# Output projection in seven block products, and the second token half first into the norm and the up projection, in a hybrid attention/SSM encoder block

## The chip, the cores and the metric

The kernel runs on one NeuronCore of a Trainium2 chip. The metric is the device time of one execution in microseconds (us). Five engines work side by side, each through its own list of instructions in order: PE (TensorE, the matmuls), DVE (VectorE), ACT (ScalarE), POOL (GpSimd) and SP (SyncE, which here only starts transfers). Matrix products write to PSUM banks; ACT or DVE carry them out.

## What is computed

1024 tokens of width 1024, with 16 meta tokens ahead of them, pass through one layer: a mixer of attention and a state-space model, its output projection, a residual, and then a norm and a gated convolution FFN. The part that is changed is the end of the mixer and the start of the FFN:

```python
def _mixer(xn, w_in, ..., w_o):
    ...
    merged = g[..., :D_MODEL] * y_a.astype(jnp.float32) + g[..., D_MODEL:] * y_s.astype(jnp.float32)
    return merged.astype(xn.dtype) @ w_o        # (tokens, 1024) @ (1024, 1024)

x = x + _mixer(_rmsnorm(x, g1), ...)
...
def _conv_ffn(xn, w_up, conv_w, conv_b, w_down):      # xn = _rmsnorm(x, norm_ffn_g)
    hid = xn @ w_up                                   # (tokens, 1024) @ (1024, 5632)
    hp = jnp.pad(hid, ((0, 0), (CONV_WIDTH - 1, 0), (0, 0)))
    conv = conv_b + sum(hp[:, j:j + seq_len] * conv_w[j] for j in range(CONV_WIDTH))
    val, gate = jnp.split(conv, 2, axis=-1)
    return (jax.nn.silu(gate) * val) @ w_down
```

All of it is float32. Of the meta tokens, the output projection needs only the last two, since the causal convolution reaches two tokens back.

## The kernel before

**How a float32 product is made.** Each operand is split in two: a rounded high part `hi` (type fp32r), and a low part `lo`, the operand minus `hi`. A product is three matmuls, hi times hi, hi times lo and lo times hi, summed in one PSUM bank. ACT makes `hi` by a cast and DVE or POOL makes `lo` by a subtraction (`split_lo`, recorded as L128 whatever calls it).

**The order.** The code is recorded once; the build's scheduler and the buffers of each pool then settle each engine's list, so that the lists are not the code line by line. Within a list an instruction that waits holds all behind it.

**The stages around the change**, in order of time:
- *Attention*, four pairs of heads. In these stages POOL makes masks, scalings and weight casts, and some transfers start on its queue.
- *Merge* (L907 on). For each of eight chunks i of 128 features, 36 matmuls multiply attention output by `w_ao`; DVE multiplies by the gate (L916) and adds the state-space part `mi` (L917); ACT casts the 128x1026 sum to `xhi`, and POOL makes `xlo`. POOL also casts the weights of a coming chunk (`whi`, L148) here.
- *Output projection* (L931 on). For two halves of 512 output columns, and for each of 8 tiles of 128 tokens, 24 matmuls of 512 columns give one bank; DVE adds it to `h2` (L955). The two meta tokens take 16 more matmuls per half (`stacked`). The split weights `woh`, `wol` come from `wo_half` (ACT cast, DVE subtraction of 128x1024), four loads of 512 KB for each half.
- *Norm*, tile by tile in the second half: ACT squares and sums, DVE forms the variance `vr`, POOL its power (`rs`, L172), DVE scales to `xs` (L177), PE transposes (L185), ACT casts to `xhi` (L187) and DVE makes `xlo`.
- *Up projection* (L1039 on). `plain_pair(0)` computes the first of 22 channel pairs: two row blocks, each in three pieces of 342 tokens with 24 matmuls each; ACT and twice DVE (L1057) carry a piece out with the convolution's taps. `xn_forms()` then makes the sums of token halves that later block products need (POOL L1072, DVE L252 to L256, and splits), `plain_pair(1)` follows, and then `block` pairs (L213 to L215 on PE), each in seven products. The weights of every pair are loaded, cast on ACT (L1002) and split on DVE.
- *Down projection*, which uses seven block products too, with operands formed on POOL, ACT and DVE.

The weights for the down projection have sums of blocks made in DRAM while other work runs: SP copies a block to `t_d` and a POOL transfer adds another (L1028).

## Time and profile before

| | |
|---|---|
| median of 3 runs | 1508.7 us (1506.5 to 1511.5) |
| the profiled execution | 1509.3 us, of which the span from first to last instruction is 1507.5 us |
| mean granted TensorE clock | 0.989 of full |
| PE | busy 1454.5 us, 96% of the span, 9736 matmuls |
| DVE | busy 1064.2 us, 71% |
| POOL | busy 714.8 us, 47% |
| ACT | busy 679.0 us, 45% |

PE is busy nearly always, so a slice in which it is not, and what it waits for there, is what one looks for first. The stages of the change take some 220 us of the span: the merge from 664 to 710 us, the output projection and the norm to 823 us, `plain_pair(0)`, `xn_forms` and `plain_pair(1)` to 868.8 us, and the `block` pairs behind that. A matmul's busy time includes its run through the pipeline, so that the distance between two starts, the pitch, tells what one costs.

### The profile page before, as it was taken

To read this page: it belongs to the slowest core of one execution; us is meant where nothing else is said; L and a number is where in the kernel's file an instruction comes from. 1 tells how busy PE (TensorE), PEld (TensorE's weight loads), DVE (VectorE), ACT (ScalarE), POOL (GpSimd) and SP (SyncE) were. 2 spreads that over 40 slices of the span, in tenths; PEclk is the share of its full clock that TensorE was granted. 3 is DMA by queue.
4 is the path that set the end of the run, shared out by engine and by line. 5 is a ranking of instruction groups with operands and counts; after the bars stand their busy time and mean duration, and the time that the engine had idled before them with its cause. 6 is when DMAs were issued, how large, how long until landed. Compare 5 with 4: busy or idle time off the path is not lost.

```text
span 1507.5 us, 26382 instructions
## 1 busy us (share of the span) xinstructions
PE 1454.5 (96%) x9736; PEld 1366.9 (91%) x9736; DVE 1064.2 (71%) x2143; ACT 679.0 (45%) x1304; POOL 714.8 (47%) x805
## 2 busy tenths in 40 slices
PE   7999998999999999999999899999999999989997
PEld 6989997998999999999778899999999999878886
DVE  7878758871657676656255988888887775788785
ACT  6344665531646565532033444444444444444343
POOL 1411135760545555525011644555544326599766
PEclk9999999999999999999999999999999999999998
DMA  6465562551021202157241136766643214864413
GB/s 242 99 161 140 142 139 80 159 166 46 21 77 54 78 23 93 43 174 264 96 165 59 54 107 162 196 188 180 166 114 96 77 62 164 309 218 131 132 49 112
DMA packets 82245, 189.92 MB, mean 126 GB/s; under 512 B 14090, under 2 KB 24970, under 8 KB 81764
## 3 DMA queue, kind: packets, MB, share of 16 engines
q1 hardware_dynamic: 66164, 154.49, 31.4%
q0 software_dynamic: 9728, 23.09, 8.4%
q10 hardware_dynamic: 6224, 10.65, 1.9%
q8 instruction: 77, 1.26, 0.3%
q14 instruction: 52, 0.43, 0.1%
HBM read 149.12 MB, written 60.96 MB: 139 GB/s over the span
## 4 chain that ended last, share of the span: by engine, by line
PE 74%; DVE 13%; issue 3%; POOL 3%; DMA 3%; ACT 3%; SPq 0%; POOLq 0%; DVEq 0%; ACTq 0%
PE mm L154 5%; PE mm L156 5%; PE mm L155 5%; PE sp L214 3%; PE sp L213 3%; PE sp L215 3%; PE tp L750 2%; DVE sw L128 2%; PE tp L213 2%; PE tp L214 2%; PE tp L215 2%; DVE ov L1093 2%; PE mm L213 2%; PE mm L215 2%; PE mm L214 2%
## 5 line engine op out<-in xcount | busy, mean ns | idle before, releaser
L154 PE MATMUL mm<-xhi,whi 128*128 128x342 f32 (+2 forms) x488 | 159.4, 327 | 1.0 <-DVE q L128 1.0
L156 PE MATMUL mm<-xhi,wlo 128*128 128x342 f32 (+2 forms) x488 | 158.3, 325 | 0.0
L155 PE MATMUL mm<-xlo,whi 128*128 128x342 f32 (+2 forms) x488 | 157.6, 323 | 0.0
L128 DVE TENSOR_TENSOR sw<-sf,sw 128x512 fp32r<-128x512 f32 x76 | 75.8, 997 | 55.1 <-ACT sw L1002 55.1
L1033 POOL TENSOR_TENSOR ov<-ov,og 128x1024 f32<-128x1024 f32 x21 | 51.2, 2440 | 129.6 <-ACT og L1032 126.8
L1002 ACT CAST sw<-sf 128x512 fp32r<-128x512 f32 x76 | 47.5, 624 | 111.4 <-POOL sf L1010 79.6
L154 PEld LDWEIGHTS mm<-xhi,whi 128*128 128x128 f32 x488 | 91.9, 188 | 2.1 <-PE sp L708 0.8
L156 PEld LDWEIGHTS mm<-xhi,wlo 128*128 128x128 f32 x488 | 91.8, 188 | 0.3
L155 PEld LDWEIGHTS mm<-xlo,whi 128*128 128x128 f32 x488 | 91.9, 188 | 0.2
L213 PE MATMUL mm<-xhi,sw 128*128 128x256 f32 (+1 forms) x304 | 85.6, 282 | 1.0 <-DVE ov L1057 1.0
L215 PE MATMUL mm<-xhi,sw 128*128 128x256 f32 (+1 forms) x304 | 85.5, 281 | 0.0
L214 PE MATMUL mm<-xlo,sw 128*128 128x256 f32 (+1 forms) x304 | 85.2, 280 | 0.0
L757 ACT CAST th<-tp 128x256 fp32r<-128x256 f32 (+3 forms) x120 | 56.0, 472 | 61.8 <-PE tp L750 29.0
L128 DVE TENSOR_TENSOR tl<-tp,th 128x256 fp32r<-128x256 f32 (+3 forms) x120 | 65.2, 547 | 25.7 <-ACT th L757 24.4
L1002 ACT CAST sw<-raw 128x512 fp32r<-128x512 f32 x69 | 42.3, 620 | 79.8 <-DMA raw<-in_w_up_dram 36.5
L1093 DVE SCALAR_TENSOR_TENSOR ov<-hv,cwt,ov 128x1024 f32<-128x1024 f32 x38 | 77.5, 2040 | 0.3 <-ACT ov L1091 0.3
L722 POOL TENSOR_SCALAR pt<-pt,nm 128x144 f32<-128x144 f32 (+4 forms) x72 | 50.7, 706 | 53.8 <-DVE nm L721 52.4
L1010 POOL TENSOR_TENSOR sf<-raw,sf 128x512 f32<-128x512 f32 x38 | 64.0, 1683 | 23.2 <-DVE sw L128 23.1
L1010 POOL TENSOR_TENSOR sf<-raw 128x512 f32<-128x512 f32 x38 | 50.1, 1318 | 48.4 <-DVE sw L128 24.1
L172 POOL TENSOR_TENSOR rs<-vr,nhalf 128x1 f32<-128x1 f32 (+2 forms) x18 | 10.9, 605 | 113.9 <-DVE vr L170 61.5
L720 ACT ACTIVATE pt<-pt,nm 128x144 f32<-128x144 f32 (+4 forms) x72 | 52.9, 735 | 26.0 <-DVE nm L719 25.5
L713 DVE CUSTOM_DVE_ANT_0 pt<-sp,fb 128x328 f32<-128x328 f32 (+8 forms) x112 | 46.4, 430 | 20.6 <-PE sp L708 12.3
(606 smaller groups left out, 5648.9 us busy)
## 6 DMA issues: line engine op xcount, KB each, us to landing
raw<-in_w_up_dram SPq DMA_DIRECT2D x44, 512.0 KB, 3.9
t_d<-in_w_dn_dram POOLq DMA_DIRECT2D x44, 256.0 KB, 6.7
ar<-a_d SPq DMA_DIRECT2D x44, 256.0 KB, 4.3
wr<-t_d SPq DMA_DIRECT2D x44, 256.0 KB, 2.8
a_d<-ov SPq DMA_DIRECT2D x21, 512.0 KB, 2.6
wr<-in_w_dn_dram SPq DMA_DIRECT2D x33, 256.0 KB, 3.4
t_d<-in_w_dn_dram SPq DMA_DIRECT2D x22, 256.0 KB, 4.5
t_d<-t_d SPq DMA_DIRECT2D x22, 256.0 KB, 4.5
```

The costliest lines, as they stand in the source:

```text
L128: return eng.tensor_tensor(out_, src, hi.bitcast(F), ALU.subtract)
L154: yield PE.matmul(ps, whi[:, i, :], ahi[:, i], start=(i == 0), stop=False)
L155: yield PE.matmul(ps, whi[:, i, :], alo[:, i], start=False, stop=False)
L156: yield PE.matmul(ps, wlo[:, i, :], ahi[:, i], start=False, stop=(i == k - 1))
L213: PE.matmul(ps, a[0][:, i], bh, start=(i == 0 and not joins), stop=False, skip_group_check=True)
L214: PE.matmul(ps, a[0][:, i], bl, start=False, stop=False, skip_group_check=True)
L215: PE.matmul(ps, a[1][:, i], bh, start=False, stop=(i == kh - 1), skip_group_check=True)
L720: S.activation(pt[:n, :kc], pt[:n, :kc], AF.Exp, bias=nm[:n, 1:2], scale=0.125, accum_out=nm[:n, 2:3])
L757: S.copy(th[:kn, z:tw], tp[:kn, z:tw])
L1002: S.copy(hi, src)
L1010: sums.append(GP.tensor_tensor(f_, a, b, op))
L1093: V.scalar_tensor_tensor(out=o, in0=h_[:, j:SEQ + j], scalar=cwc(j, m), in1=o, op0=ALU.mult, op1=ALU.add)
```

## The change

The output projection is written as a 2 by 2 block product (token halves by feature halves by column halves) in seven products instead of eight, with sums of blocks as operands.

- **Products.** Each has 4 tiles of 128 tokens with 12 matmuls of 512 columns: 7 x 4 x 12 = 336, where there were 384. The meta tokens take four small products of 8 matmuls (32 as before). On PE the order is 0, 4, 1, 5, 2, 3, 6; products 4, 5 and 6 go on in the banks of 0, 1 and 3. DVE adds or subtracts each finished bank to `h2` (L1021 of after) and POOL adds product 2 to three more places, in 12 instructions.
- **Operands.** The eight merged tiles are kept in float32. POOL forms the token sums (16 of 128x512), ACT casts token and weight blocks of 128x512 (56), and the low parts are made on POOL for products 0, 4 and 5 and on DVE for 1, 2, 3 and 6. The operands of 0, 5 and 3 stand in the memory of `xhi`, those of 4 and 2 in that of `xlo`. `wo_half` is gone.
- **Weight sums.** Four blocks `to_d` of 512x512 are made in DRAM during the second and third pair of heads: four copies by SP and four accumulating transfers by POOL, 1 MB each.
- **Norm.** The last four token tiles are normed during product 6, then the meta tokens, then the first four tiles. The squares go into the buffer of `xs`.
- **Up projection.** `plain_pair(0)` is computed in two parts, each of two pieces of 254 to 258 tokens: the second token half, then the first. That is 192 matmuls of 256 to 260 columns, where there were 144 of 342 to 344.

The core of the diff:

```diff
+    def out_weight_sums(i, first):
+        steps = [[(3, o_block(0, 0), False), (1, o_block(0, 1), False)],
+                 [(3, o_block(0, 1), True), (1, o_block(1, 1), True)],
+                 [(2, to_d[3], False)], [(2, o_block(1, 1), True)], [(5, to_d[2], False)], [(5, o_block(1, 0), True)]]
+        for p, src, more in steps[i] if i < len(steps) else ():
+            d_ = GP.dma_start(to_d[p], src, accum_op=ALU.add) if more else SY.dma_start(to_d[p], src)
+            after(d_, first)
...
+    def out_forms(p, j):
+        a11, a21, a12, a22 = (merged[4 * k + j][:, 2 + 512 * h_:514 + 512 * h_] for k in range(2) for h_ in range(2))
+        sub, add = ALU.subtract, ALU.add
+        if p == 1:
+            GP.tensor_tensor(a11, a11, a21, sub)
+        elif p == 2:
+            GP.tensor_tensor(a11, a22, a11, add)
+        elif p == 3:
+            GP.tensor_tensor(a21, a22, a21, sub)
+        elif p == 6:
+            GP.tensor_tensor(a11, a11, a12, sub)
+        slot = slots_of[p][j]
+        for q, src in ((0, (a11, a11, a11, a21, a12, a22, a11)[p]), (2, wr.pop((p, j)))):
+            S.copy(slot[q], src)
+            split_lo(GP if p in (0, 4, 5) else V, slot[q + 1], src, slot[q])
...
         V.tensor_tensor(mi, mi, ga, ALU.add)
-        S.copy(xhi[:, i, T0:], mi)
-        split_lo(GP, xlo[:, i, T0:], mi, xhi[:, i, T0:])
-        if i == 1:
-            wo = [wo_half(wop, 0, mg, "wraw")]
+        out_forms((0, 4)[i // 4], i % 4)
...
-                for i in range(KD):
-                    PE.matmul(ps, xhi[:, i, t:t + n], woh[:, i], start=(i == 0), stop=False)
-                    PE.matmul(ps, xhi[:, i, t:t + n], wol[:, i], start=False, stop=False)
-                    PE.matmul(ps, xlo[:, i, t:t + n], woh[:, i], start=False, stop=(i == KD - 1))
-            V.tensor_tensor(dst[:, sl], ps[:n], dst[:, sl], ALU.add)
...
+        for i, (ah, al, bh, bl) in enumerate(slots_of[p]):
+            k_ = dict(skip_group_check=True)
+            PE.matmul(ps, ah[:, ts_], bh, start=(i == 0 and p not in JOINS), stop=False, **k_)
+            PE.matmul(ps, ah[:, ts_], bl, start=False, stop=False, **k_)
+            PE.matmul(ps, al[:, ts_], bh, start=False, stop=(i == 3), **k_)
+        if p == 0:
+            S.copy(to, ps)
+        else:
+            V.tensor_tensor(to, to, ps, ALU.subtract if p in MINUS else ALU.add)
+        if p == 2:
+            for d_, op in ((bot[:, l_], ALU.add), (bot[:, r_], ALU.subtract), (top[:, r_], ALU.subtract)):
+                GP.tensor_tensor(d_, d_, u2[t], op)
...
+    for p in (0, 4, 1, 5, 2, 3, 6):
+        for t in range(4):
+            out_product(p, t)
+            if p == 6:
+                normed(5 + t, h2[:, 4 + t], P)
...
+    normed(0, hm, 2)
+    for t in range(4):
+        normed(1 + t, h2[:, t], P)
...
-    plain_pair(0)
+    plain_pair(0, ([(514, 256), (770, 254)], [(0, 258), (258, 256)]))
     xn_forms()
     plain_pair(1)
```

**POOL in the merge stage.** Before, a weight cast `whi` and the low part of a merged chunk took turns:

```order
L148 TENSOR_SCALAR whi_8786<-raw_8784 128x512
L128 TENSOR_TENSOR xlo_91<-mi_8654,xhi_90 128x1026
L148 TENSOR_SCALAR whi_8841<-raw_8839 128x512
L128 TENSOR_TENSOR xlo_91<-mi_8727,xhi_90 128x1026
L148 TENSOR_SCALAR whi_8896<-raw_8894 128x512
```

In the changed kernel, in the same stage (`wr` is a raw weight block of the output projection, `mr` a merged tile, L931 a token sum for product 1, L935 one for product 3):

```order
L129 TENSOR_TENSOR xhi_94<-mr2_8510,xhi_94 128x512
L931 TENSOR_TENSOR mr2_8510<-mr2_8510 128x512
L149 TENSOR_SCALAR whi_8906<-raw_8904 128x512
L129 TENSOR_TENSOR xhi_94<-mr3_8511,xhi_94 128x512
L931 TENSOR_TENSOR mr3_8511<-mr3_8511 128x512
L149 TENSOR_SCALAR whi_8964<-raw_8962 128x512
L935 TENSOR_TENSOR mr0_8508<-mr4_8512,mr0_8508 128x512
L129 TENSOR_TENSOR xlo_95<-mr4_8512,xlo_95 128x512
L149 TENSOR_SCALAR whi_9018<-raw_9016 128x512
L935 TENSOR_TENSOR mr1_8509<-mr5_8513,mr1_8509 128x512
```

Token sums now stand between the weight casts on POOL.

**DVE at the end of the norm.** Before, the last low parts stand among the first evictions of `plain_pair(0)` (L1057), and the first subtraction of `xn_forms` (L252) follows:

```order
L128 TENSOR_TENSOR xlo_91<-sp_9698,xhi_90 128x4x128
L177 SCALAR_TENSOR_TENSOR xs_9739<-h2_9059,rs_9745,g2B_9082 128x1024
L128 TENSOR_TENSOR xlo_91<-tp_9705,xhi_90 128x4x128
L1057 SCALAR_TENSOR_TENSOR og_9799<-mm_9800,cwt_9770,og_9799 128x342 x2
L128 TENSOR_TENSOR xlo_91<-sp_9748,xhi_90 128x4x128
L128 TENSOR_TENSOR xlo_91<-tp_9755,xhi_90 128x4x128
L1057 SCALAR_TENSOR_TENSOR og_9799<-po_9828,cwt_9770,og_9799 128x342 x2
L252 TENSOR_TENSOR fb_9981<-fa_9980 128x514
```

In the changed kernel, at the same place (L1171 is the eviction, L254 the first subtraction):

```order
L129 TENSOR_TENSOR xlo_95<-sp_9847,xhi_94 128x4x128
L129 TENSOR_TENSOR xlo_95<-tp_9854,xhi_94 128x4x128
L1171 SCALAR_TENSOR_TENSOR og_9897<-mm_9898,cwt_9868,og_9897 128x256
L1171 SCALAR_TENSOR_TENSOR og_9897<-mm_9926,cwt_9868,og_9897 128x254
L1171 SCALAR_TENSOR_TENSOR og_9897<-mm_9898,cwt_9868,og_9897 128x256
L1171 SCALAR_TENSOR_TENSOR ov_9962<-mm_9963,cwt_9868,ov_9962 128x256
L1171 SCALAR_TENSOR_TENSOR og_9897<-mm_9926,cwt_9868,og_9897 128x254
L1171 SCALAR_TENSOR_TENSOR ov_9962<-po_9991,cwt_9868,ov_9962 128x254
L1171 SCALAR_TENSOR_TENSOR ov_9962<-mm_9963,cwt_9868,ov_9962 128x256
L1171 SCALAR_TENSOR_TENSOR ov_9962<-po_9991,cwt_9868,ov_9962 128x254
L254 TENSOR_TENSOR fb_10135<-fa_10134 128x514
```

All eight evictions of the second token half now stand behind the last low part and ahead of the first subtraction.

**DVE ahead of the norm.** In the changed kernel, after the low parts of product 3's operands, the up projection's weight splits (`sw`) stand among the evictions of product 2 (`u2`) and ahead of those of product 3 (`h2`), and the norm's `vr` and `xs` behind them:

```order
L1021 TENSOR_TENSOR u2_9077<-u2_9077,mm_9462 128x512
L129 TENSOR_TENSOR sw_9891<-raw_9889,sw_9891 128x512
L129 TENSOR_TENSOR sw_9894<-raw_9889,sw_9894 128x512
L129 TENSOR_TENSOR sw_9956<-raw_9954,sw_9956 128x512
L129 TENSOR_TENSOR sw_9959<-raw_9954,sw_9959 128x512
L1021 TENSOR_TENSOR u2_9077<-u2_9077,po_9463 128x512
L129 TENSOR_TENSOR sw_10208<-raw_10206,sw_10208 128x512
L129 TENSOR_TENSOR sw_10211<-raw_10206,sw_10211 128x512
L129 TENSOR_TENSOR sw_10301<-raw_10299,sw_10301 128x512
L129 TENSOR_TENSOR sw_10304<-raw_10299,sw_10304 128x512
L1021 TENSOR_TENSOR h2_9082<-h2_9082,mm_9537 128x512
L172 TENSOR_SCALAR vr_9620<-ss_9618 128x1
```

Before, such splits stood at the start of the norm too, among the evictions of the projection's second half:

```order
L128 TENSOR_TENSOR sw_10054<-raw_10052,sw_10054 128x512
L128 TENSOR_TENSOR sw_10057<-raw_10052,sw_10057 128x512
L170 TENSOR_SCALAR vr_9344<-ss_9342 2x1
L128 TENSOR_TENSOR sw_10147<-raw_10145,sw_10147 128x512
L955 TENSOR_TENSOR h2_9059<-mm_9363,h2_9059 128x512
L128 TENSOR_TENSOR sw_10150<-raw_10145,sw_10150 128x512
L177 SCALAR_TENSOR_TENSOR xs_9340<-hm_9084,rs_9346,g2B_9082 2x1024
L170 TENSOR_SCALAR vr_9393<-ss_9391 128x1
```

The splits keep their place at the head of the norm; ahead of product 3's evictions they are new.

## Rows read from the trace of the kernel before

**Rows 1.** The page: span, busy times of the engines.

```profile
span 1507.5 us, 26382 instructions
PE 1454.5 (96%) x9736; PEld 1366.9 (91%) x9736; DVE 1064.2 (71%) x2143; ACT 679.0 (45%) x1304; POOL 714.8 (47%) x805
```

**Rows 2.** Busy time by stretch of the span, us; columns in the first line.

```profile
core 0: us, PE busy (x) PEld busy (x) DVE busy (x) ACT busy (x) POOL busy (x), PEclk, DMA share, GB/s
440.00:460.00 20.00, 19.66 (x146) 18.76 (x145) 10.92 (x55) 10.30 (x32) 12.12 (x28) 1.00 0.28 85
...
664.00:710.00 46.00, 45.80 (x294) 45.52 (x292) 32.85 (x43) 12.57 (x13) 23.72 (x15) 1.00 0.71 233
710.00:814.00 104.00, 102.67 (x471) 81.55 (x472) 44.18 (x63) 26.15 (x45) 11.14 (x14) 1.00 0.36 133
...
829.00:878.00 49.00, 42.94 (x271) 42.39 (x270) 48.64 (x60) 24.57 (x42) 29.82 (x20) 0.93 0.20 55
...
986.00:1026.00 40.00, 40.00 (x339) 40.00 (x338) 33.09 (x42) 17.34 (x28) 21.93 (x19) 1.00 0.70 185
```

**Rows 3.** Timeline of PE: start us, duration us, instruction, [idle before <-releaser].

```profile
705.75 0.32 PE L915 MATMUL mm<-ohi,wlo 128*128 128x342 f32 x1
...
709.48 0.32 PE L915 MATMUL po<-ohi,wlo 128*128 128x342 f32 x1
710.50 0.48 PE L952 MATMUL po<-woh,xhi 128*128 128x512 f32 x1 [0.70 <-DVE gs L916]
710.81 0.40 PE L953 MATMUL po<-wol,xhi 128*128 128x512 f32 x1
...
715.93 0.40 PE L954 MATMUL po<-woh,xlo 128*128 128x512 f32 x1
...
822.21 0.60 PE L185 MATMUL sp<-ident,xs 128*128 128x128 f32 x4
822.64 0.60 PE L185 MATMUL tp<-ident,xs 128*128 128x128 f32 x4
...
859.14 0.62 PE L1051 MATMUL mm<-xhi,sw 128*128 128x344 f32 x1 [4.50 <-DVE og L1057]
```

**Rows 4.** Timeline of DVE at the end of the norm.

```profile
814.56 0.69 DVE L955 TENSOR_TENSOR h<-mm,h 128x512 f32<-128x512 f32 x1 [1.11 <-PE mm L954]
...
817.81 1.27 DVE L177 SCALAR_TENSOR_TENSOR xs<-h,rs,g2B 128x1024 f32<-128x1024 f32 x1
...
824.07 0.68 DVE L128 TENSOR_TENSOR xlo<-tp,xhi 128x512 fp32r<-128x512 f32 x1
...
829.32 1.78 DVE L252 TENSOR_TENSOR fb<-fa 128x514 f32<-128x514 f32 x1 [3.48 <-POOL fa L1072]
```

**Rows 5.** Groups of DVE and POOL, 655 to 845 us: busy us, mean ns | idle before.

```profile
L128 DVE TENSOR_TENSOR sw<-raw,sw 128x512 fp32r<-128x512 f32 x10 | 7.2, 742 | 4.1 <-ACT sw L1002 4.1
L1057 DVE SCALAR_TENSOR_TENSOR ov<-mm,cwt,ov 128x342 f32<-128x342 f32 x4 | 2.2, 563 | 0.0
...
L128 POOL TENSOR_TENSOR xlo<-mi,xhi 128x1026 fp32r<-128x1026 f32 x8 | 16.3, 2033 | 20.6 <-ACT xhi L918 20.6
L1072 POOL TENSOR_TENSOR fa<-xhi,xlo 128x514 f32<-128x514 f32 x6 | 8.5, 1437 | 7.5 <-DVE xlo L128 6.9 <-DVE t3l L128 0.6
L148 POOL TENSOR_SCALAR whi<-raw 128x512 fp32r<-128x512 f32 x7 | 8.2, 1175 | 15.4 <-PE po L155 13.0 <-PE mm L914 2.2
```

**Rows 6.** The same groups in the down projection, 1280 to 1508 us.

```profile
L128 DVE TENSOR_TENSOR op<-wr,op 128x512 fp32r<-128x512 f32 x15 | 19.4, 1301 | 1.1 <-ACT op L1159 1.1
...
L128 POOL TENSOR_TENSOR op<-wr,op 128x512 fp32r<-128x512 f32 x15 | 22.9, 1536 | 0.0
L1153 POOL TENSOR_TENSOR ar<-ar 128x512 f32<-128x512 f32 x11 | 17.1, 1561 | 5.4 <-DVE xlo L128 3.0 <-DVE xhi L128 2.5
```

**Rows 7.** Groups of POOL over the span: issue of its accumulating transfers.

```profile
L1028 POOL DMA_DIRECT2D t_d<-in_w_dn_dram x44 | 36.8, 1179 | 0.0
```

**Rows 8.** Timeline of POOL within the attention stage: a weight cast, scaling and split.

```profile
449.93 1.05 POOL L148 TENSOR_SCALAR whi<-raw 128x1024 fp32r<-128x1024 f32 x1 [2.33 <-PE mm L155]
450.95 1.05 POOL L440 TENSOR_SCALAR gs<-gs 128x1026 f32<-128x1026 f32 x1
451.98 2.38 POOL L128 TENSOR_TENSOR wlo<-raw,whi 128x1024 fp32r<-128x1024 f32 x1
```

More of the change, by code (lines that the diff above doesn't have):

```diff
@@ L930, in block_kernel @@
+    u2t = [n2.tile([P, 2, 512], F, tag="xs", name="u2", bufs=2) for _ in range(2)]
+    u2 = [t_[:, i] for t_ in u2t for i in range(2)]
+    hm = n2.tile([2, D], F, name="hm")
+    mstk = n2.tile([P, 12, 64], R, name="mstk")
+    md = n2.tile([P, 12, 2], F, name="md")
+    ml = n2.tile([2, 512], F, name="ml")
     h2 = n2.tile([P, KD, D], F, name="h2")
-    SY.dma_start(h2, x.rearrange("(c p) d -> p c d", p=P))
-    wop1 = pool(st_o, "wo1", side="right")
-    wo.append(wo_half(wop1, 1, wp, "raw"))
@@ new lines, in block_kernel, with meta_product @@
+    small = [n2.tile([P, 4, 512], R, name=f"op{q}") for q in range(4)]
+    slots_of[1] = slots_of[6] = [[t_[:, w] for w in range(4)] for t_ in small]
+    GP.memset(mstk.bitcast(F), 0.0)
+    for i in range(KD):
+        GP.tensor_copy(md[:, i], merged[i][:, :2])
+    GP.tensor_tensor(md[:, KD:], md[:, :4], md[:, 4:KD], ALU.subtract)
+    GP.tensor_copy(mstk[:, :, :2], md)
+    split_lo(GP, mstk[:, :, 32:34], md, mstk[:, :, :2])
+    HALF = [slice(0, 512), slice(512, D)]
+    def meta_product(ps, q, p, start=True, stop=True):
+        for i, (_, _, bh, bl) in enumerate(slots_of[p]):
+            PE.matmul(ps[:64], mstk[:, 4 * q + i], bh, start=start and i == 0, stop=False, skip_group_check=True)
+            PE.matmul(ps[:64], mstk[:, 4 * q + i], bl, start=False, stop=stop and i == 3, skip_group_check=True)
@@ new lines, in normed, with operands @@
+    def normed(c, dst, n):
+        xs = n2.tile([P, D], F, tag="xs", name="xs", bufs=2)
+        norm_rows(n2, dst, n, g2B, xs)
+        to_feature(xs, n, xhi, xlo, TILES[c][0] if c else T0)
+        if c:
+            SY.dma_start(h_d[P * (c - 1):P * c], dst)
+    after_of = {None: (1,), 0: (5,), 4: (2,), 5: (3, 6)}
+    tags = {1: "raw", 5: "whi", 2: "wlo", 3: "raw", 6: "whi"}
+    def operands(p):
+        for nx in after_of.get(p, ()):
+            for q in range(2):
+                out_weights(nx, q, wp, tags[nx])
+            for j in range(4):
+                out_forms(nx, j)
@@ new lines, in block_kernel @@
+    operands(None)
+    xc = x.rearrange("(c p) d -> p c d", p=P)
+    SY.dma_start(h2[:, :4], xc[:, :4])
+    for p in (0, 4, 1, 5, 2, 3, 6):
[3 more added lines that the diff above has]
+                normed(5 + t, h2[:, 4 + t], P)
+        if p == 0:
+            xy = t_ps()
+            meta_product(xy, 0, 0)
+            meta_out(xy, HALF[0])
+            GP.tensor_tensor(hm[:, HALF[1]], hm[:, HALF[1]], ml, ALU.subtract)
+        elif p == 4:
+            xy = t_ps()
+            meta_product(xy, 1, 4)
+            meta_out(xy, HALF[0])
+        elif p == 2:
+            xy = s_ps()
+            meta_product(xy, 1, 2, stop=False)
+        elif p == 3:
+            meta_product(xy, 2, 3, start=False)
+            meta_out(xy, HALF[1])
+        operands(p)
+        if p == 0:
+            SY.dma_start(h2[:, 4:], xc[:, 4:])
@@ L1037, in conv_out, with plain_pair @@
         return ha.tile([P, SEQ], F, tag=tag, name=tag)
[L1039 removed]
+    def plain_pair(c, parts=(QBLK,)):
         res = []
[L1041 to L1045 removed]
+        ws = {}
+        for part, (m, tag) in ((part, mt) for part in parts for mt in ((NFF + c, "og"), (c, "ov"))):
+            if m not in ws:
+                raw = up_raw(m)
+                ws[m] = [split_q(raw[:, KH * q:KH * q + KH]) for q in range(2)]
+                res.append(conv_out(m, tag))
+            w2, o = ws[m], res[len(ws) - 1 if len(ws) < 2 else int(m == c)]
+            for t, n in part:
                 w = min(n, SEQ - t)
@@ L1180, in banks @@
         return held[p]
-    HALF = [slice(0, 512), slice(512, D)]
     ss = {}
```

113 lines of the change are left out of this document (52 added, 61 removed).

## The prediction

> **What bounds the kernel now.** I read the page first: PE is busy for 1454.5 of 1507.5 us [rows 1], so the span shrinks where PE gets less to do, unless another engine takes over there. Next the busy time by stretch [rows 2]. In the merge stage (664 to 710 us) and in the output projection (710 to 814) PE is full, 45.80 of 46 and 102.67 of 104 us, while DVE has 32.85 and 44.18: PE bounds both. From 829 to 878 us it is the other way: DVE is busy 48.64 of 49 us, PE 42.94, at a granted clock of 0.93. Here `xn_forms` and the evictions of two plain pairs bound the kernel. The timelines show the same: PE waits 4.50 us at 859.14 for an eviction on DVE [rows 3], and DVE itself begins this work at 829.32, after 3.48 us of waiting for POOL's first sums [rows 4], which need the last low part of the norm (824.07 + 0.68 = 824.75).
>
> So the change takes its matmuls from a stretch that PE bounds, but just behind it stands one that DVE bounds, and whose start depends on the end of the norm. What counts is how much earlier the last low part is ready.
>
> **PE's own sum.** Starts of 512-column matmuls are (715.93 - 710.81) / 22 = 0.2327 us apart [rows 3]. 416 such matmuls become 368: 48 x 0.2327 = 11.2 us less. `plain_pair(0)` has 192 matmuls instead of 144. The 342-column pitch is (709.48 - 705.75) / 24 = 0.1555, the pitch near 256 columns 40.00 / 339 = 0.118 [rows 2, 3]: 22.7 against 22.4 us, 0.3 more. The 0.70 us of idle at 710.50 [rows 3], a wait for the last gated chunk, goes, since product 0 needs chunks 0 to 3 alone. PE alone would thus gain 11.2 + 0.7 - 0.3 = 11.6 us.
>
> **When the last low part is ready.** The merge ends at 709.8 (709.48 + 0.32). Up to product 6 PE has (6 x 48 + 32) x 0.2327 = 74.5 us, so that product 6 starts at 784.3. It takes 11.2 and the transposes of two token tiles, each two groups of (822.64 - 822.21) = 0.43 to 0.44 us [rows 3], 0.88 in all: 797.2. Then follow the transposes of two more tiles (1.8), the first part of `plain_pair(0)` (96 x 0.118 = 11.3) and, among its matmuls, those of the meta tokens (0.2) and of four tiles (3.5). Last transposes: start at 813.1 by PE's order alone.
>
> They wait for the scaled tile, though. Its buffer `xs` exists twice, and in the changed kernel the squares are written into it too, so a tile's square cannot start before the tile two ahead is transposed; for the last one this is about 811.5. From the end of an eviction to the end of `xs` the old norm took 817.81 + 1.27 - (814.56 + 0.69) = 3.83 us [rows 4]: 815.4. From the start of the last transposes to the last low part it took 824.75 - 822.21 = 2.54 [rows 3, 4]. That gives 817.9.
>
> DVE may not keep up with this. Between product 5's end (709.8 + 208 x 0.2327 = 758.2) and 797.2 it has 24 operand and weight splits (8 each for products 3 and 6 and for the up projection, whose splits stand ahead of product 3's evictions), 16 evictions and two norms. At 0.742 us a split [rows 5], 0.69 an eviction and about 2.8 a norm (1.27 and two of 0.68 [rows 4], and the variance) this is 17.8 + 11.0 + 5.6 = 34.4 of 39.0 us. The split of two SBUF operands costs more when POOL is busy: in the down projection it is 1.301 us [rows 6]. POOL has 12 additions and 4 sums in this stretch, about 16 x 1.5 = 24 us [rows 5, 6], six tenths of it, so up to 24 x 0.56 x 0.6 = 8 us more on DVE, some 3.5 to 5 beyond what fits. Hence 817.9 to 823; I take the middle, 820.5, since DVE has waits for PE among these instructions that absorb a part. Against 824.75 the norm ends 4.2 us earlier.
>
> **What is then late next.** Before, DVE waited 3.48 us for POOL's sums [rows 4]. Now it has all eight evictions of the second token half queued in front, 8 x some 0.5 us (0.563 at 342 columns [rows 5]) = 4 us: they fill that wait and no more. The DVE-bound stretch starts 4.2 us earlier and holds slightly less, since eight evictions at 0.56 are eight at about 0.48: 0.6 us. Gain where it reaches the block stage: **4.8 us**, bounds 2.4 and 7.4 (823 and 817.9). The rest of PE's 11.6 us becomes idle time on PE: waits for `xs`, for PSUM banks whose evictions stand behind the norm, and for `xn_forms`.
>
> **What it costs elsewhere.** *Merge stage.* POOL has 23.72 us of work in 46 [rows 2]. Now: 8 weight casts at 1.175, 15 operand splits at 1.02 (half of the 2.033 for 1026 columns) and 7 token sums at about 1.44 [rows 5]: 9.4 + 15.3 + 10.1 = 34.8 us. ACT exchanges casts of equal length, and DVE loses the four 128x1024 splits of `wo_half`. A weight cast for the next chunk now stands behind a sum and a split. Here PE waits if the cast is late, and its cover is a chunk's 36 matmuls, 5.6 us. Bounds: nothing, or one sum and one split at their dearer price, 1.56 + 1.54 = 3.1 us [rows 6]. I take **1.5 us**.
>
> *Attention.* Four accumulating transfers are added to POOL's queue; masks and scalings that scores wait for are behind them. The nearest row is L1028, 1.179 us for 128 rows of 2 KB [rows 7]. These have 512 rows: 4.7 us together if the price is per transfer, 18.9 if per row. The trace holds POOL bursts of that size: 449.93 to 454.36 us is one of 4.4 us [rows 8], and PE is busy 19.66 of 20 us around it [rows 2]. At that rate four cost 4 x 0.34 = 1.4; bounds 0 and 6; I take **1 us**. SP's four copies stand in a queue that computes nothing, and the loads of the next weights stand behind them, ahead of their use.
>
> The Trainium skill, page "DMA: Bandwidth & Descriptors", section "Anatomy of one DMA — SWDGE (gpsimd) path", has the cost of generating descriptors on this path grow little until a transfer has many of them. By that, POOL would spend the 4.7 us, not the 18.9, and the 1 us would be nearer to nothing.
>
> **Sum.** -4.8 + 1.5 + 1.0 = -2.3 us. Against the profiled execution (1509.3) 1507.0. The median of the runs is 0.6 lower, so 1506.4; I forecast **1506.5 us**, with 1502.5 to 1510.5 from the bounds of its terms. A measurement of this kernel tells about 0.3%, 4.5 us, from no change, so that the forecast is a change that cannot be told.
>
> **Rival 1: PE's gain arrives.** If DVE keeps up and the norm ends as PE's order allows (last transposes at 813.1, last low part at 815.6), the DVE-bound stretch starts 9.1 us earlier. With its 0.6 and a part of the idle 4.50 us [rows 3] regained, since PE's work lies better against DVE's, this is 10 to 13 us; less 1 to 2 of costs, 1497 to 1500, range 1494 to 1502. For it: PE bounds the stretch before (102.67 of 104). Against: DVE's 34.4 of 39 us and the two `xs` buffers.
>
> **Rival 2: POOL and DVE cannot supply operands (slower).** The place is the merge stage. At the dearer prices [rows 6] POOL has 9.4 + 15 x 1.54 + 7 x 1.56 = 43.4 of 46 us, and its token splits still follow ACT's casts of a chunk: in the old order it idled 20.6 us on those [rows 5]. If half of that idle time remains, 10 us, POOL needs 53 and the stage lasts 7 us longer, because PE's weights come from POOL. It decides from POOL work and waits of 46 us together on. Operands of products 3 and 6 are late for the same reason, and the norm's gain is 2.4. Then 1509.3 + 7 + 1 - 2.4 - 0.6 = 1514, and up to 1519 if the attention stage pays 6. For it: rows of the down projection, where both engines make such operands at once. Against: there POOL hardly idles, while it is only half busy here.
>
> The Trainium skill, page "SBUF — State Buffer", section "SBUF: two separate sides", calls the port pair that VectorE and GpSimd share an exclusive lock, so that a VectorE instruction with two SBUF inputs blocks for the whole of a GpSimd instruction. Rows 5 and 6 agree in kind (0.742 against 1.301 us). By that rule alone each of product 3's eight splits could stand behind a POOL instruction, 8 x (0.68 + 1.3) = 15.8 us, and end at 774 us while PE wants them at 771: it speaks for this rival.
>
> **Rival 3: nothing shifts.** The norm ends where it did, since DVE's queue sets it, and the small costs remain: 1508 to 1511. This lies within "cannot be told" as well.
>
> **Chances.** The forecast with rival 3: 0.55, of which 0.10 falls below 1504.2 and 0.05 above 1513.2. Rival 1: 0.25, all faster. Rival 2: 0.20, nearly all slower. Faster by over 0.3%: 0.35; within: 0.41; slower: 0.24. For 8 in 10 the range takes in most of rival 1 and the lower half of rival 2: 1497 to 1515.
>
> **What would show it.** Output projection: PE's stretch from the last merge matmul to the end of product 6 about 87 us. The last low part of the norm about 111 us after the merge's end (820.5 on the old clock), and the first subtraction of `xn_forms` 4 to 5 us behind it. DVE full for 48 us from there. Rival 1 shows in a last low part 106 us behind the merge; rival 2 in a merge stage of over 50 us with PE waiting for `whi`. I am wrong in kind if POOL's transfers stop PE during attention by more than 6 us, or if PE idles for operands between products by more than 5.

## The result, and the profile after

The changed kernel takes 1516.0 us (median, 1512.4 to 1519.6) where the kernel before took 1509.7 beside it: ratio 1.0044, interval 1.0028 to 1.0060. It is slower by some 6.6 us, where the forecast had it 2.3 us faster, a change that cannot be told. The profiled execution took 1517.7 us, its span is 1515.9.

The page: PE's busy time fell by 6.8 us against [rows 1], its span grew by 8.4. PE's idle time is now 68.2 us, before 53.0.

```profile
span 1515.9 us, 26588 instructions
PE 1447.7 (96%) x9736; PEld 1363.6 (90%) x9736; DVE 1093.1 (72%) x2178; ACT 697.6 (46%) x1351; POOL 782.2 (52%) x866
```

Busy time by stretch, with the columns of [rows 2]; the third row of figures is the merge stage alone, from its first matmul to the end of its last:

```profile
core 0: us, PE busy (x) PEld busy (x) DVE busy (x) ACT busy (x) POOL busy (x), PEclk, DMA share, GB/s
440.00:460.00 20.00, 19.66 (x148) 18.91 (x147) 10.39 (x51) 8.62 (x24) 11.02 (x25) 1.00 0.33 95
...
829.00:878.00 49.00, 37.25 (x223) 36.65 (x224) 45.93 (x59) 21.25 (x36) 31.68 (x21) 0.79 0.15 43
...
668.69:719.82 51.13, 47.54 (x291) 46.82 (x290) 28.59 (x38) 10.03 (x17) 37.19 (x38) 0.97 0.63 219
```

The merge stage lasts 51.13 us instead of 45.12 (664.68 to 709.80, PE full). 3.6 us of the 6.0 are idle time on PE, 2.4 are matmuls that took longer. Timeline of PE from the merge to the second pair, the places where it waits for more than 2 us:

```profile
685.99 0.32 PE L960 MATMUL mm<-ohi,wlo 128*128 128x342 f32 x1
689.74 0.65 PE L958 MATMUL mm<-k,whi 128*128 128x342 f32 x1 [3.43 <-POOL whi L149]
690.19 0.49 PE L959 MATMUL mm<-k,whi 128*128 128x342 f32 x1
...
692.84 0.33 PE L958 MATMUL mm<-ohi,whi 128*128 128x342 f32 x1
...
756.85 0.50 PE L1015 MATMUL sp<-xhi 128*128 128x512 f32 x1 [2.77 <-DVE h L1021]
...
757.65 0.57 PE L1015 MATMUL tp<-op 128*128 128x512 f32 x1
...
761.00 0.45 PE L1017 MATMUL tp<-op 128*128 128x512 f32 x1
...
829.57 1.09 PE L187 MATMUL sp<-ident,xs 128*128 128x128 f32 x4 [2.56 <-DVE xs L179]
...
834.18 0.56 PE L1165 MATMUL mm<-xhi,sw 128*128 128x260 f32 x1 [2.67 <-DVE og L1171]
...
872.05 0.63 PE L1165 MATMUL mm<-xhi,sw 128*128 128x344 f32 x1 [8.51 <-DVE og L1171]
```

Two of these waits are new in stretches that PE bounded: one for a weight of the merge (`whi`), and one for the bank in which product 5 goes on from product 1. Each costs more than its idle time in this profile. From 689.74 to 692.84 the 11 starts are 10 steps of 0.31 us on average, in [rows 3] 0.1555: 1.5 us more. From 757.65 to 761.00 the 8 steps are 0.42 us each instead of 0.2327: 1.5 us more. The granted clock of these two stretches is 0.50 and 0.51: the lower of TensorE's two levels, 1.2 instead of 2.4 GHz.

The fall of the clock behind the bank wait does not come every time. In a second profile of the same kernel (e12 below) PE waits as long for the bank, the granted clock stays at 1.00, and the 11 steps from 755.10 to 757.61 are 0.23 us each:

```profile
754.30 0.50 PE L1015 MATMUL sp<-xhi 128*128 128x512 f32 x1 [2.77 <-DVE h L1021]
...
755.10 0.40 PE L1015 MATMUL tp<-op 128*128 128x512 f32 x1
...
757.61 0.40 PE L1017 MATMUL tp<-op 128*128 128x512 f32 x1
```

What POOL did while PE waited for `whi`:

```profile
672.49 6.26 POOL L129 TENSOR_TENSOR xhi<-wr,xhi 128x512 fp32r<-128x512 f32 x4 [0.87 <-ACT xhi L940]
678.72 0.61 POOL L149 TENSOR_SCALAR whi<-raw 128x512 fp32r<-128x512 f32 x1
679.31 1.08 POOL L129 TENSOR_TENSOR xhi<-mr,xhi 128x512 fp32r<-128x512 f32 x1
680.36 1.74 POOL L129 TENSOR_TENSOR xlo<-wr,xlo 128x512 fp32r<-128x512 f32 x1
682.05 2.29 POOL L931 TENSOR_TENSOR mr<-mr 128x512 f32<-128x512 f32 x1
684.30 3.75 POOL L129 TENSOR_TENSOR xlo<-wr,xlo 128x512 fp32r<-128x512 f32 x3
688.02 1.08 POOL L129 TENSOR_TENSOR xhi<-mr,xhi 128x512 fp32r<-128x512 f32 x1
689.08 0.61 POOL L149 TENSOR_SCALAR whi<-raw 128x512 fp32r<-128x512 f32 x1
```

Between the two weight casts stand four splits `xlo<-wr`, 1.74 + 3.75 = 5.5 us. They are the low parts of product 4's weights, of which the first is needed when product 4 starts, 11 us behind the merge. The planner, which is the build's scheduler, placed them there; that it did so because the weights had arrived by then is my reading. POOL is not full (37.19 of 51.13 us): the cast is late by its place in the queue. It starts 20.4 us behind the start of the merge, the same cast 12.2 us before the change, and PE wants the weight at 17.6.

DVE ahead of the bank wait, and from the last low part of the norm to the first subtraction:

```profile
743.19 4.51 DVE L129 TENSOR_TENSOR xlo<-mr,xlo 128x512 fp32r<-128x512 f32 x3
747.63 0.68 DVE L1021 TENSOR_TENSOR h<-h,po 128x512 f32<-128x512 f32 x1
748.23 1.19 DVE L129 TENSOR_TENSOR xlo<-mr,xlo 128x512 fp32r<-128x512 f32 x1
749.34 6.86 DVE L129 TENSOR_TENSOR xlo<-wr,xlo 128x512 fp32r<-128x512 f32 x4
756.12 0.67 DVE L1021 TENSOR_TENSOR h<-h,sp 128x512 f32<-128x512 f32 x1
...
832.17 0.69 DVE L129 TENSOR_TENSOR xlo<-tp,xhi 128x512 fp32r<-128x512 f32 x1 [0.16 <-ACT xhi L189]
...
837.11 1.76 DVE L254 TENSOR_TENSOR fb<-fa 128x514 f32<-128x514 f32 x1 [1.13 <-POOL fa L1185]
```

The eviction that PE wants, the one at 756.12, stands behind five splits for product 2, and the last four take 1.7 us each. POOL's sums for product 6 run at the same time:

```profile
748.82 6.82 POOL L937 TENSOR_TENSOR mr<-mr,mr 128x512 f32<-128x512 f32 x4
```

**Where the 8.4 us of the two profiled spans are.** 3.1 are there at 225 us already, ahead of everything that the change touches; over thirteen traces the first matmul behind that point lies between 223.1 and 229.4 us, so this is no effect. From there to the merge 440.0 us instead of 439.1: +0.9, with a spread of 437.2 to 440.0 over the traces. Merge +6.0. From the merge's end to the first matmul of the down projection 569.1 instead of 569.4: -0.3, where -4.8 was expected. Down projection -1.3. A second profile of the changed kernel (e12 below) has the same shape with +0.1, +5.7, -2.6 and +0.9.

### The profile page after: what moved, and what is told of

The parts are those of the page before. It is cut to its first block, busy times and chain, and to the rows that moved or that the text cites. A ratio compares the mean times of both kernels' runs of the same rounds, so it can differ in the third digit from the quotient of the medians.

```text
span 1515.9 us, 26588 instructions
## 1 busy us (share of the span) xinstructions
PE 1447.7 (96%) x9736; PEld 1363.6 (90%) x9736; DVE 1093.1 (72%) x2178; ACT 697.6 (46%) x1351; POOL 782.2 (52%) x866
## 4 chain that ended last, share of the span: by engine, by line
PE 78%; DVE 9%; DMA 6%; issue 3%; POOL 2%; ACT 2%; SPq 0%; POOLq 0%; DVEq 0%; ACTq 0%
PE mm L155 4%; PE mm L157 4%; PE mm L156 4%; PE sp L215 4%; PE sp L216 4%; PE sp L217 4%; PE mm L215 3%; PE tp L215 3%; PE mm L217 3%; PE tp L216 3%; PE mm L216 3%; PE tp L217 3%; PE tp L752 2%; PE po L774 1%; PE po L773 1%
## 5 line engine op out<-in xcount | busy, mean ns | idle before, releaser
L129 DVE TENSOR_TENSOR sw<-sf,sw 128x512 fp32r<-128x512 f32 x76 | 70.7, 931 | 52.5 <-ACT sw L1113 52.5
L724 POOL TENSOR_SCALAR pt<-pt,nm 128x144 f32<-128x144 f32 (+4 forms) x72 | 51.6, 729 | 50.7 <-DVE nm L723 49.7
L1206 DVE SCALAR_TENSOR_TENSOR ov<-hv,cwt,ov 128x1024 f32<-128x1024 f32 x38 | 74.2, 1953 | 0.2
L129 DVE TENSOR_TENSOR sw<-raw,sw 128x512 fp32r<-128x512 f32 x69 | 57.6, 842 | 3.5 <-ACT sw L1113 2.6
```

What stands on the lines that cost most here:

```text
L129: return eng.tensor_tensor(out_, src, hi.bitcast(F), ALU.subtract)
L1206: V.scalar_tensor_tensor(out=o, in0=h_[:, j:SEQ + j], scalar=cwc(j, m), in1=o, op0=ALU.mult, op1=ALU.add)
```

## The experiments

Ratios are to the kernel before, run on the same chip. "Last low part" is the end of the last `xlo` of the norm, "the forms" are the sums of token halves that `xn_forms` makes; times are counted from the end of the merge, as the prediction counts them. The last low part comes at 114.95 us before the change, at 113.0 and 110.7 in the two profiles of the changed kernel.

**Is it the amount of POOL's work?** The low parts of the weights of products 0 and 4 go to DVE:

```diff
-            split_lo(GP if p in (0, 4, 5) else V, slot[q + 1], src, slot[q])
+            split_lo(GP if p == 5 or p in (0, 4) and q == 0 else V, slot[q + 1], src, slot[q])
```

> The changed kernel, with the low parts of the weight blocks of products 0 and 4 made on DVE instead of POOL in the merge stage (8 splits); nothing else. My theory: the merge stage takes 51.1 instead of 45.1 us because these splits (6.26 us for four, 5.5 us for the other four) stand ahead of a weight cast whi on POOL, for which PE waits 3.43 us and then runs at half clock. Then the wait goes, the merge takes 45 to 46.5 us, and the time falls by 4 to 6 us from that of the changed kernel, to about 1510 to 1512 us. Rival: the merge is long because the loads of eight m_d tiles and weight blocks crowd the transfers, or because POOL's token sums and splits fill it: then PE still waits there and the merge stays at 49 us or more.

1515.2 us, ratio 1.0043 [1.0025, 1.0061], where 1510 to 1512 us was expected. The stages are read from the same kernel once more:

> The kernel of e1 once more, to see where its time goes. Its merge stage should lose the 3.43 us wait for whi, yet its time (ratio 1.0043 to the old kernel) is that of the changed kernel (1.0044). First theory: the splits moved to DVE wait there for the weight blocks' loads, and hold the evictions of the gated chunks behind them, so that PE waits 3 to 6 us for PSUM banks in the same stage. Second: the merge falls to 45 to 46.5 us and the gain is lost behind it, since the DVE-bound stretch after the norm ends when it did; then the distance from the end of the merge to the start of the down projection grows from 569.1 to 573 us or more.

1514.3 us, 1.0032 [1.0018, 1.0046]; merge stage 50.6 us. POOL and, behind it, PE:

```profile
682.73 1.42 POOL L129 TENSOR_TENSOR xhi<-mr,xhi 128x512 fp32r<-128x512 f32 x1 [2.97 <-ACT xhi L940]
684.23 1.26 POOL L931 TENSOR_TENSOR mr<-mr 128x512 f32<-128x512 f32 x1
685.46 1.20 POOL L149 TENSOR_SCALAR whi<-raw 128x512 fp32r<-128x512 f32 x2
```

```profile
686.13 0.42 PE L958 MATMUL mm<-k,whi 128*128 128x342 f32 x1 [2.47 <-POOL whi L149]
```

Eight splits fewer on POOL, which even idles 2.97 us, and PE still waits for `whi`: the cast stands behind a token split, and that waits for ACT's cast of a chunk whose sums on DVE are now behind DVE's new splits. POOL's busy time in the merge is 24.6 us here, against 37.2. The amount of POOL's work is not the cause. What stands in front of the cast is.

**Product 2's sums on POOL** (the 12 additions of `u2` into other blocks) left out:

```diff
-        if p == 2:
-            for d_, op in ((bot[:, l_], ALU.add), (bot[:, r_], ALU.subtract), (top[:, r_], ALU.subtract)):
-                GP.tensor_tensor(d_, d_, u2[t], op)
```

> The changed kernel without POOL's 12 additions of product 2 to the other three blocks (part of the output projection is left out). My theory: DVE's splits of two SBUF operands wait for POOL's instructions. In the changed kernel the eight splits of the up projection's weights take 5.79 and 6.29 us for four while POOL runs these additions (18.70 us for 12), and the evictions of product 3, and so the norm, wait behind them. Without the additions the splits take 0.6 to 0.75 us each, product 3's first eviction starts some 6 us earlier against the end of the merge (67.5 instead of 73.5 us), and the last low part of the norm is 2 to 5 us earlier than the 113.0 us after the merge's end. Time 2 to 5 us below the changed kernel. Rival: the norm's end is set by PE's order and the two xs buffers: then the splits get shorter but the last low part moves by less than 1 us and the time by less than 1.5 us.

1515.9 us, 1.0046 [1.0030, 1.0062]: no change. The up projection's weight splits on DVE in the changed kernel, and without these additions:

```profile
780.75 5.79 DVE L129 TENSOR_TENSOR sw<-raw,sw 128x512 fp32r<-128x512 f32 x4
...
787.06 6.29 DVE L129 TENSOR_TENSOR sw<-raw,sw 128x512 fp32r<-128x512 f32 x4
793.27 0.68 DVE L1021 TENSOR_TENSOR h<-h,mm 128x512 f32<-128x512 f32 x1
```

```profile
781.26 2.49 DVE L129 TENSOR_TENSOR sw<-raw,sw 128x512 fp32r<-128x512 f32 x4
...
788.11 0.68 DVE L1021 TENSOR_TENSOR h<-h,mm 128x512 f32<-128x512 f32 x1
```

A split takes 0.62 us without POOL's additions beside it, 1.45 to 1.57 with them, and product 3's first eviction moves from 73.5 to 67.7 us behind the merge. Yet the last low part moves by only 0.8 us, to 112.3, as the rival in the expectation has it. DVE's load in this stretch does not set the norm's end.

**The weight's sums in DRAM** left out, so that products 1, 2, 3 and 5 read blocks of the weight as they are:

```diff
-                out_weight_sums(4 * (pr - 1) + n_unit // 2 - 1, marks[-1])
+                pass
```

> The changed kernel without the sums in DRAM: products 1, 2, 3 and 5 read one block of w_o in their place, so no copies and no accumulating transfers run during attention (the output projection is computed with wrong weights). My theory: these cost 0.9 us (the distance from the changed kernel's to the old one's PE grew from 3.1 to 4.0 us between 357 and 480 us), and the 3.1 us before that are not the change's, since no instruction of it runs earlier. Then the stretch from 225 us to the start of the merge is 0.5 to 1.5 us shorter than in the changed kernel and the time 0 to 2 us less. Rival: the transfers slow attention and the start of the merge more widely, 3 us or more.

1514.5 us, 1.0036 [1.0020, 1.0053]; from 225 us to the merge 439.2 us. Against the changed kernel this is 0 to some 1 us. The group of POOL's accumulating transfers in the changed kernel agrees:

```profile
L815 POOL DMA_DIRECT2D to_d<-in_w_o_dram x4 | 4.3, 1067 | 3.8 <-DMA to_d<-in_w_o_dram 2.4 <-DMA to_d<-to_d 1.3 <-issue 0.2
```

**The order of the first pair.** First in the changed kernel:

```diff
-    plain_pair(0, ([(514, 256), (770, 254)], [(0, 258), (258, 256)]))
+    plain_pair(0)
```

> The changed kernel with the first pair of the up projection over the whole token range again (three pieces of 342 tokens, as before), the norm's order unchanged; PE then has no matmuls of the up projection between the transposes of the norm. My theory: what follows the norm is bound by DVE and starts with the last low part; PE's 96 matmuls (11.3 us) and eight evictions between only delay it. Then the last low part comes 2 to 5 us earlier than 113.0 us after the merge's end, and the time is 0 to 4 us below the changed kernel. Rival: those matmuls fill a gap of PE that bounds: then the time is 5 to 11 us above it.

1518.6 us, 1.0067 [1.0046, 1.0088]. The last low part comes at 108.7, and DVE is done with the forms at 162.0 instead of 167.4 (165.3 in e12), but the block pairs' first eviction on DVE (`u<-sp,c`) follows 4.1 us behind that, not 1.0. The time is 2.6 us above the changed kernel's, not 0 to 4 below. PE takes up the second pair at the old place, 868.67 - 716.70 = 152.0 us behind the merge (in the changed kernel 872.05 - 719.82 = 152.2):

```profile
868.67 0.62 PE L1165 MATMUL mm<-xhi,sw 128*128 128x344 f32 x1 [6.64 <-DVE og L1171]
```

So the earlier norm was lost again in front of the block pairs. Then the other way, the kernel before with that order and nothing else (token halves of the norm and of the pair exchanged as in the diff of the change):

> The old kernel with only the order changed: in the second column half of the output projection the last four token tiles come first, then the meta tokens and the first four, and the first pair of the up projection is computed in pieces of 254 to 258 tokens, the second token half first. No seven products, no sums in DRAM. My theory: the norm's end stays within 2 us of 115 us after the merge's end, since PE has the same work ahead of it and 96 matmuls (11.3 us) of the up projection now stand ahead of the last transposes while the norm keeps its pace: last low part 115 to 119 us, eight evictions ahead of the first subtraction as in the changed kernel; time 0 to 3 us above the old kernel. Rival: the order itself is the loss: over 5 us slower. Rival: it fills PE's idle 4.50 us: 3 us or more faster.

1509.2 us, 1.0009 [0.9993, 1.0024]: no change. Last low part 114.1, and PE's one large wait grew from 4.50 [rows 3] to 6.35 us. The stretch of DVE from the first subtraction to the last form of the four channel tiles is 48.4 us before, 48.2 with the whole pair in the changed kernel, but 50.5 here, and 50.1 in the changed kernel: with this order it is 2 us longer, with or without the block products.

**The two waits.** Product 4's weight splits on POOL wait for the sums of the later chunks:

```diff
+            lo_ = split_lo(GP if p in (0, 4, 5) else V, slot[q + 1], src, slot[q])
+            if p == 4 and q:
+                after(lo_, added[-1])
...
+        added.append(V.tensor_tensor(mi, mi, ga, ALU.add))
```

> The changed kernel, with POOL's splits of product 4's weight blocks placed one by one behind the sums of merged chunks 4 to 7, instead of all four ahead of the weight cast of chunk 3; POOL still makes them. My theory: PE's 3.43 us wait in the merge comes from those four splits ahead of the cast; then it goes, the merge takes 45 to 47 us instead of 51.1, and if the gain is not lost behind it, the time is 3 to 6 us below the changed kernel (1510 to 1513 us). Rival (POOL is simply too full in this stage): PE waits for another weight cast and the merge stays at 49 us or more.

1506.0 us (1499.9 to 1511.1), 0.9985 [0.9967, 1.0002]; merge stage 46.2 us, and no wait on `whi`. Its profile is of its shortest run, so the trace tells the places and the ratio the size. POOL has the same splits, sums and casts in the merge as in the changed kernel:

```profile
669.82 0.61 POOL L149 TENSOR_SCALAR whi<-raw 128x512 fp32r<-128x512 f32 x1
...
677.45 1.20 POOL L149 TENSOR_SCALAR whi<-raw 128x512 fp32r<-128x512 f32 x2
...
684.31 0.62 POOL L149 TENSOR_SCALAR whi<-raw 128x512 fp32r<-128x512 f32 x1 [0.17 <-PE po L962]
...
690.25 1.29 POOL L129 TENSOR_TENSOR xlo<-wr,xlo 128x512 fp32r<-128x512 f32 x1
```

The first split of product 4's weights now comes some 20 us after the last of product 0's, and none stands in front of the casts that are urgent: the one for which PE waited starts 16.8 us behind the start of the merge, not 20.4. The wait for the bank went too, which I had not planned, so that the ratio of this run is that of both. In the re-planned queue of DVE the eviction stands ahead of the last split and runs 33.8 us behind the merge instead of 36.3; PE wants the bank at 34.3 (753.68 + 0.40 - 719.82, the end of its last matmul ahead of the wait in the changed kernel).

```profile
735.47 5.17 DVE L129 TENSOR_TENSOR xlo<-wr,xlo 128x512 fp32r<-128x512 f32 x3
740.57 0.67 DVE L1024 TENSOR_TENSOR h<-h,sp 128x512 f32<-128x512 f32 x1
```

The bank alone, by product 2's operands placed between the evictions of product 1:

```diff
+            if p == 2 and j:
+                after(lo_, evicted[j - 1])
...
-    after_of = {None: (1,), 0: (5,), 4: (2,), 5: (3, 6)}
+    after_of = {None: (1,), 0: (5,), 1: (2,), 5: (3, 6)}
```

> The changed kernel, with the splits of product 2's operands on DVE placed between the evictions of product 1 instead of ahead of them. My theory: in the changed kernel eight such splits (12.5 us, slowed by POOL's instructions) hold product 1's first eviction back to 756.1 us, and PE waits 2.77 us for that bank before product 5 and runs at half clock for 3 us behind it. Then this wait goes, products end 86 to 88 us after the merge's end instead of 90.4, the last low part comes 109 instead of 113 us after it, and the time is 2 to 4 us below the changed kernel. Rival: the norm or product 2 waits instead (operands late): the last low part stays within 1 us of 113.

1509.8 us, 1.0015 [1.0000, 1.0030]. No wait for the bank, last low part 107.6; the merge stage is as long as in the changed kernel (51.5 us, with 3.08 us of waiting for `whi`). Both edits together:

> The changed kernel with both reorderings: the splits of product 4's weights behind the sums of merged chunks 4 to 7 (as e6) and the splits of product 2's operands between the evictions of product 1 (as e8). In e6 the wait of 2.77 us for product 1's bank was gone without the second one, in e8 the wait for whi remained. My theory: both waits cost the changed kernel some 5 and 4 us; e6 already had both back, so that this is e6 within 1.5 us: merge 46 to 47 us, last low part 106.5 to 109 us behind it, time 1503 to 1507 us, ratio to the old kernel 0.996 to 0.999. Rival: the two gains add up because the waits have separate causes: 1501 us or less.

1504.9 us, 0.9978 [0.9964, 0.9992]: by this ratio some 3 us faster than the kernel before. Merge 46.5 us, last low part 107.7. Against e8, which differs by the first edit alone, the wait for `whi` is worth 0.0037 of the time, 5.6 us.

**The scaled tile's buffers.** On top of both edits, the squares of the meta tokens and of four tiles go to operand tiles that are free by then, not into `xs`:

```diff
-        norm_rows(n2, dst, n, g2B, xs)
+        norm_rows(n2, dst, n, g2B, xs, flat(small[c % 4])[:, :D] if c < 5 else None)
```

> As e9, and for the meta tokens and the first four token tiles the norm's squares go to the finished operand tiles of product 6, not into the buffer of xs, so that a square need not wait until the tile two ahead is transposed. My theory: with the two waits gone, the pace of these norms (a wait of 2.67 us of PE for the last xs) comes from this buffer; then that wait shrinks below 1 us, the last low part comes 1.5 to 3 us earlier than in e9, and the time is 0 to 3 us less, since the stretch that DVE bounds starts earlier. Rival: DVE and POOL set the pace of the norm themselves: last low part and time within 1 us of e9.

1502.6 us, 0.9960 [0.9945, 0.9976], the best of these kernels. The last low part comes at 105.3, PE's wait of 2.56 us for the last `xs` in e9 is gone, and its large wait is 4.73 us instead of 7.93. In e9 and here:

```profile
858.06 0.63 PE L1173 MATMUL mm<-xhi,sw 128*128 128x344 f32 x1 [7.93 <-DVE og L1179]
```

```profile
852.30 0.63 PE L1173 MATMUL mm<-xhi,sw 128*128 128x344 f32 x1 [4.73 <-DVE og L1179]
```

This gain did not come through an earlier end of the forms: the stretch of DVE takes 53.1 us instead of 49.7, and they end at 162.9, in e9 at 161.9. In the re-planned queue of DVE the evictions stand further ahead among the forms, and PE takes up the second pair at 138.3 instead of 146.7; the down projection starts 2.2 us earlier. How much of this is due to the buffers and how much to the new order of the queue was not tested.

With the whole first pair on top of that:

> As e10, with the first pair of the up projection over the whole token range again (as e4 on the changed kernel). It tells what computing the second token half first is worth once the two waits are gone. In e4 the last low part came 4.4 us earlier, but the start of the down projection only 1.4 us, and the time was above that of the changed kernel. My theory: PE then idles during the norm and owes 11 us of matmuls after it, while DVE starts its stretch 2 to 4 us earlier; the two nearly cancel: 0 to 4 us above e10, ratio to the old kernel 0.996 to 0.999. Rival: PE bounds this stretch once the norm is early: 5 us or more above e10. Rival: DVE alone bounds it: 2 us or more below e10.

1504.3 us, 0.9973 [0.9962, 0.9984]. The last low part comes 4.8 us earlier still (100.5) and the forms are done 8 us earlier, but PE's large wait is 7.33 us and it takes up the second pair at 143.9, later than in e10. The first eviction of the block pairs is again 4.1 us behind the forms. The down projection starts 1.7 us earlier than in e10 in the traces, and nothing of that shows in the time:

```profile
857.93 0.63 PE L1173 MATMUL mm<-xhi,sw 128*128 128x344 f32 x1 [7.33 <-DVE og L1179]
```

Beside it the changed kernel ran once more:

> The changed kernel once more, unaltered, beside e11 and the old kernel: the merge takes 51 to 51.6 us with the wait of 3.4 us for whi, PE waits 2.77 us for product 1's bank, the last low part comes 110.5 to 113.5 us after the merge's end; ratio 1.003 to 1.006. The 3.1 us by which its first profile was later already at 225 us should not come back as a rule: 225.5 to 229.5 us there, as in the other runs.

1514.0 us, 1.0037 [1.0023, 1.0050], with the same waits as the first profile: 2.75 us for `whi` (3.43 in the first), 2.77 for the bank, 2.56 for `xs`, 2.82 and 8.79 for `og`.

## Why the prediction was wrong

**Merge stage, +1.5 (0 to 3.1): mis-sized, and the largest part of the miss.** It measured +6.0 and +5.7, outside its bounds in both profiles. The step that failed is "Here PE waits if the cast is late, and its cover is a chunk's 36 matmuls": I counted POOL's work (34.8 of 46 us; 37.2 measured in 51.1) and bounded a late cast by one sum and one split in front of it. In front stood also the four splits of weights for a product that comes much later, 5.5 us. The POOL lines above show them there. And an idle stretch was priced at its length, where 2.4 us of slower matmuls come on top.

**Rival 2: right in place, wrong in mechanism.** A merge stage of over 50 us with PE waiting for `whi` is what it named. It decided by POOL's work and waits together passing 46 us. e5 takes work from POOL and keeps the wait; e6 keeps the work and loses the wait. With its own price of 7 us for the merge it gave 1514 and more, near what was measured, but the remedy that follows from it, another engine for the splits, did nothing.

The Trainium skill, page "SBUF — State Buffer", section "SBUF: two separate sides", has a VectorE instruction with two SBUF inputs blocked while a GpSimd instruction that reads SBUF holds the port pair that they share. e2's splits (0.62 against 1.45 to 1.57 us) and the 1.7 us splits ahead of the bank wait agree in kind. The rule tells that the splits get dear, not whether that costs time. In front of product 3 it cost none (e2). Ahead of the bank the five splits took 8.0 us; at 0.62 us each they would take 3.1, which is an estimate from these rows, and the 4.9 us between exceed the 2.77 us of the wait. That POOL's sums alone made the bank late was not tested.

**Between the products: not foreseen.** PE idles 2.77 us for the bank and in the first profile runs 1.5 us longer behind it; "more than 5" was my mark for an error in kind, and it stayed under that. By its removal alone (e8) 3.3 to 4.4 us come back by the ratios, which is the idle time and, in some executions, the slow matmuls.

**Last low part at 110.7 (108.1 to 113.2): the number held by luck, its reason did not.** Measured 113.0 and 110.7. I put it 2.6 us above what PE's order and the `xs` buffers give (108.1) because DVE would be over-full. DVE was dear there as estimated (12.1 us for eight splits), and e2 shows that this does not count. What filled the 2.6 us and more is the bank wait: without it the last low part comes at 107.6, 107.7 and 108.8 (e8, e9, e6), the 108.1 of the bound. e10 confirms the `xs` buffers as the limit: it moves them out of the way and gains 2.4 us there.

The two profiles of the changed kernel differ by 2.3 us here, and the place is the clock. In the first it falls behind the bank wait, 1.5 us, and again at the last transposes (1.09 us for four, before 0.60 [rows 3]); in the other it stays at 1.00 in both places. Why the same wait lets the clock fall once and not the other time is open.

**DVE's stretch, 0.6 us shorter: wrong sign.** The first subtraction follows 4.3 us behind the last low part, as forecast (4 to 5), and the 20 evictions in the stretch that follows are 0.7 us shorter, also as forecast. But it takes 50.1 us instead of 48.4: the 16 forms 19.3 instead of 18.3 us, the 16 splits of their parts 17.1 instead of 15.8. e4 and e7 point to the order of the pair, but not to one kind of work: in e7 it is nine weight splits with 11.4 us, where eight took 8.1. That evictions, which read PSUM, used to lie beside POOL's work and splits lie there now is my reading; it was not tested. So of the 4.8 us at the block stage 0.5 and 2.6 arrived. In the second profile, where the norm ends as forecast, this stretch alone makes the difference; in the first it shares it with the later norm.

**Attention, +1 (0 to 6): right, and at the low end.** +0.9 and +0.1 in the traces, 0 to 1 by e3. In the first profile the four transfers of 512 rows take 1.05 to 1.09 us of POOL each, a transfer of 128 rows took 1.179 [rows 7]: here the price is per transfer.

The Trainium skill, page "DMA: Bandwidth & Descriptors", section "Anatomy of one DMA — SWDGE (gpsimd) path", says that many descriptors can be emitted before their cost shows up. The trace agrees: 4.3 us, where 4.7 were estimated for a price per transfer and 18.9 for one per row.

**PE's own 11.6 us: right that they do not arrive as a whole.** Busy time fell by 6.8 us, since slower matmuls took a part of the 11.2 back, and idle time grew by 15.2. Rival 1 asked for a last low part at 106 and 1497 to 1500 us. e10 has it at 105.3 and takes 1502.6, e11 at 100.5 and takes 1504.3: even where the norm ends as early as that, what lies between it and the block pairs takes most of the gain.

**The sum.** Forecast -4.8 + 1.5 + 1.0 = -2.3. By the two profiles: -0.3 to -2.6 for the block stage, +6.0 to +5.7 for the merge, +0.9 to +0.1 for attention, which is +6.6 and +3.2; the runs have +6.6 and +5.6. In the first profile the merge and the block stage miss by 4.5 us each, in the second by 4.2 and 2.2. The range of the terms, up to 1510.5, ends 5.5 us short of the measured 1516.0, and the wide one, up to 1515, by 1: the merge's bound of 3.1 left out whatever else the planner puts in front of a cast, and the block stage's bound of 2.4 a stretch of DVE that grows.

**What the change is worth** without the two waits: e9 against e7, which has the new order alone, -4.7 us; with the `xs` buffers free (e10) -7.4. These are differences of ratios, and the interval of each ratio is some 2 us to either side. Whether the new order of the first pair costs or brings anything stays open: by the ratios e4 and the two runs of the changed kernel differ by 3.5 and 4.5 us in its favour, e11 and e10 by 2.0, with intervals that overlap, and e7 by 1.4 us against it.

## What to carry to other kernels

When work moves to an engine with idle time, read in its new queue what stands in front of each instruction that the bottleneck waits for; the sum of the work against the length of the stage says nothing about it. Work whose result is needed late can be held back by an explicit dependence; here the planner had put it ahead of what was urgent, and one such line brought 5 to 6 us back. Where a bottleneck's work is cut, follow each later stage to its first result: here an earlier norm was lost twice in front of the same block pairs.
